# A hybrid state-space and attention layer: TensorE in program order through the projections, turns and parameter products put off by two units

## The chip, the core and the metric

The kernel runs on one core of a Trainium2 chip. The core's engines are TensorE (PE in the rows below, with PEld for its weight loads), VectorE (DVE), ScalarE (ACT), GpSimd (POOL) and SyncE (SP), which here issues DMA transfers only. They run side by side and wait for each other by semaphores; each takes its own instructions in order. The metric is the device time of one launch in microseconds (us).

## What is computed

One layer over 1024 latent tokens and 256 context tokens of width 1024. The normed and modulated input goes through one projection to Q, K, V, U and the gates. U feeds an S5 branch (a complex diagonal state-space model in 32 groups of 16 channels, scanned in both directions), Q, K and V a differential attention with 8 heads. The two branches are merged by the gates, then a gated MLP with a depthwise convolution follows. Cut to what matters here:

```python
z = modulate(x, p['norm1_w'], sh1, sc1) @ w_in
q = rms_norm(z[..., Q_OFF:K_OFF].reshape(b, l, N_HEADS, 2, HEAD_DIM), p['q_norm_w'])
k = rms_norm(z[..., K_OFF:V_OFF].reshape(b, l, N_HEADS, 2, HEAD_DIM), p['k_norm_w'])
v, u, g = ...                       # V_OFF:U_OFF, U_OFF:G_OFF, G_OFF:
q, k = rope_2d(q, rope), rope_2d(k, rope)
y_attn = diff_head_out(blocked_latent_diff_attention(q, k_all, v_all, lam), ...)
y_s5, y_s5_c = s5_branch(u, uc, p, update_ctx)   # discretise, scan, C s + D u, GELU, GLU
x = x + ga1 * merge_branches(g, y_s5, y_attn, p['b_gate'], p['w_out'])
x = x + ga2 * conv_ffn(modulate(x, p['norm2_w'], sh2, sc2), ...)
```

## The kernel before

The part that the change touches is the first third of the program, `phase_a` and what follows it up to the scores of the attention (about 760 us). It works in **units**: `project(tt, W)` multiplies one tile of 128 tokens by one slab of 512 columns of the input projection into a PSUM tile `z` (five of them). Every fp32 product is split into a high part and a rest (`whi`, `wlo` for weights, `hTh`, `hTl` for the input), and three products are added, so that a unit is 8 x 3 = 24 matmuls (L417, L418, L419). A slab's weights come by DMA into `wraw` in four quarters; ScalarE makes `whi`, GpSimd `wlo` (L608).

The units come in this order: U (10 tiles), K in two slabs `s` = 0, 1 (20 units), V in two (20), Q in two (16, latent tokens only). After a unit of K or Q, `qk_post` does the norm and the rotation: ScalarE squares, VectorE reduces over each head (L653), takes a root in a few small steps (L654 to L661) and forms two products with the tables (L665, L669), GpSimd adds them and scales a part, ScalarE scales the rest (L675, L676), and then TensorE **turns** the result: 8 transpositions into `ta` and `tb` (L680).

Between units, three other pieces of work are stepped on as generators. `gates` makes the gates in 32 **halves** of 24 matmuls each (L1308 to L1310 through the helper `gemm`; the same lines serve other products). `s5_params` makes, for each of 8 groups q of the S5 branch (`QUADS`), the matrices `ba`, `ca`, `blk`, `dup` on VectorE or GpSimd, transposes `ba` (L863) and multiplies `ca` with `blk` (L881). `s5_scan` is the scan on VectorE (L959 to L962); `s5_states_in` feeds it during V; `ada_part` computes the second and third part of the adaLN vectors in 16 k-steps a group, each of them two products per half, in row groups of 32 (L300).

When Q is done, the remaining gate halves are made in turn with `s5_out_quad` (8 of them), whose results `Yq` are turned and written to DRAM as `Yd`. The S5 branch's end then loads them as `y` (four quarters, one buffer), applies the GELU on ScalarE, splits into `h5h` (VectorE, L1300) and `h5l` (GpSimd, L1301) and multiplies with the GLU weights into `ta` and `tb` (L1308). Then come the scores `sc` from `K` and `q`.

What sets the order: each engine's instructions are ordered at build time by a scheduler that keeps its own timeline of all engines and puts an instruction where it expects it to be ready. It may so shift the turns, gate halves and parameter products of TensorE between the matmuls of units. Program order decides only where the scheduler sees a tie, or where a part is marked as manual. Pools with a number of buffers (the last argument of `self.t`) limit how far a piece may run ahead.

Of the kernel before, what the change touches and what calls it, by code (L numbers as in the profile page):

```python
# [13 lines left out]
OP = mybir.AluOpType  # L14
# [23 lines left out]
QUADS = G // 4  # L38
# [101 lines left out]
class Kern:  # L140
# [149 lines left out]
    def ada_part(self, pool, ps, crep, grp):  # L290

        nc = self.nc
        pa = self.t(ps, [P, 512], "ada", 1)
        for k in range(KT):
            for h in range(2):
                a = self.t(pool, [P, 2, 512], "araw", 2)
                nc.sync.dma_start(a, self.I["ada"][grp - 1, k][:, 2 * h:2 * h + 2])
                for z in range(2):
                    r0 = 32 * (2 * h + z)
                    nc.tensor.matmul(pa[r0:r0 + 32], crep[:, k], a[:, z], start=k == 0, stop=k == KT - 1,  # L300
                                     tile_position=(0, r0))
# [12 lines left out]
        yield  # L314

    def phase_a(self):
# [180 lines left out]
        for tt in range(NKT):  # L497
            u = stage(first[tt] if tt < TA else project(tt, W))
            if tt < NT:
                nc.scalar.dma_start(self.Ud[:, tt], u)  # L500
            else:
                nc.scalar.dma_start(self.Ucd[(tt - NT) * P:(tt - NT + 1) * P], u)
            if tt % 2:
                next(params, None)
        zp, zp_st = self.pool("pk")
        self.rope_tables(zp, "K")
        gates = self.gates(wp, ps, hTh, hTl)
        for s in (0, 1):
            W = self.load_slab(wp, s)
# [6 lines left out]
        zp_st.close()  # L516
        for _ in params:
            pass
        xp, xp_st = self.pool("s5x")
        states = self.s5_states_in(xp, ps)  # L520
        next(states)
        scan = self.s5_scan()
        for s in (2, 3):
            W = self.load_slab(wp, s)
            for tt in range(NKT):
                v = stage(project(tt, W))
                nc.scalar.dma_start(self.Vd[tt][:, (s - 2) * 512:(s - 1) * 512], v)
                if s > 2 or tt > 1:
                    if next(states, True):
                        next(scan, None)  # L530
        hc_st.close()
        ap_, ap_st = self.pool("pada", "right")
        zp, zp_st = self.pool("pq")
        self.rope_tables(zp, "Q")
        adas = (st for grp in (1, 2) for st in self.ada_part(ap_, ps, crep, grp))
        for s in (5, 6):
            W = self.load_slab(wp, s)
            for tt in range(NT):
# [5 lines left out]
                next(scan, None)  # L544
# [6 lines left out]
        for _ in gates:  # L551
            next(adas, None)
            if nq < QUADS:
                if nq % 2 == 0:
                    Yq = self.t(yp, [P, NT, P], "Yq", 1)
                with self.tc.high_priority():
                    self.s5_out_quad(yp, ps, nq, Yq, xp)
                    nq += 1
                    if nq % 2 == 0:
                        self.s5_transpose(yp, ps, Yq, nq // 2 - 1)  # L560
                if nq == QUADS:
                    for _ in adas:
                        pass
                    ap_st.close()
                    yp_st.close()
                    xp_st.close()
                    tail = self.s5_tail(ps)
            else:
                next(tail, None)
# [43 lines left out]
    def rope_tables(self, zp, kind):  # L613

        nc, I = self.nc, self.I
        tp, tp_st = self.pool("rope")
        cs = self.t(tp, [P, 2, NT, HD], "cossin")
# [13 lines left out]
        tp_st.close()  # L631
# [14 lines left out]
    def qk_post(self, zp, ps, pz, kind, hs, tt):  # L646
# [15 lines left out]
        t1 = self.t(zp, [P, 8, HD], "t1", 2)  # L662
        if tt < NT:
            ct, st = self.tabs[kind]
            nc.vector.tensor_tensor(t1, zv, ct[:, None, tt].to_broadcast([P, 8, HD]), op=OP.mult)  # L665
            t2 = self.t(zp, [P, 8, 2, 32], "t2", 2)
# [9 lines left out]
        nc.gpsimd.tensor_tensor(t1[:, na:], t1[:, na:], r[:, na:, None].to_broadcast([P, 8 - na, HD]), op=OP.mult)  # L676
        pt = self.pst([P, 4, P])
# [93 lines left out]
    def s5_params(self, ps):  # L771
# [62 lines left out]
        for q in range(QUADS):  # L834
            yield
            E = nc.vector if q % 2 or q == 6 else nc.gpsimd
            gs = slice(4 * q, 4 * q + 4)
            sb = self.t(sp, [P, 2, 4, GC], "sb", 1)
            sc = self.t(sp, [P, 2, 4, GC], "sc", 1)
# [7 lines left out]
            ba = self.t(sp, [P, 2, 4, 8, GC], "ba", 1)  # L847
            ca = self.t(sp, [P, 2, 4, 8, GC], "ca", 1)
# [10 lines left out]
            nc.sync.dma_start(self.Wod[q], ca.rearrange("p i g s c -> p i g (s c)"))  # L859
            for i in range(2):  # L860
                pt = self.t(ps, [P, 4, P], "ada", 1)
# [6 lines left out]
            blk = self.t(sp, [P, 2, 2, 4, 2, GC], "blk", 1)  # L868
            nc.gpsimd.memset(blk, 0.0)
            dup = self.t(sp, [P, 2, 4, 2, GC], "dup", 1)  # L870
            V.tensor_copy(dup, bb[:, :, :, None].to_broadcast([P, 2, 4, 2, GC]))
            for d_ in range(2):
                rs = slice(64 * d_, 64 * d_ + 64)
                V.tensor_copy(blk[rs, d_], bb[rs, :, :, None].to_broadcast([64, 2, 4, 2, GC]))
            V.tensor_scalar(sc[:, 1], sc[:, 1], -1.0, None, op0=OP.mult)
            pk = self.t(ps, [P, 272], "ada", 1)
# [12 lines left out]
            nc.sync.dma_start(self.Td[q], kq)  # L889
        sp_st.close()  # L890
# [681 lines left out]
```

## Time and profile before

| | us |
|---|---|
| median of 3 runs (lowest, highest) | 2135.11 (2131.05, 2136.24) |
| the profiled execution, its span | 2132.76, 2131.0 |
| TensorE busy in the span | 2045.3 (96%) |
| VectorE, GpSimd, ScalarE busy | 1161.1, 825.9, 785.5 |
| mean granted TensorE clock | 0.987 of full speed |

A share of busy time is a mean over stages with different limits, so the stages are read one at a time below. Busy time of TensorE counts a matmul that runs at half clock as busy for twice as long; the granted clock beside it tells which it was.

### The profile page before, as it was taken

What the parts mean: (1) busy time and instruction counts of PE and PEld (TensorE: products, weight loads), DVE (VectorE), ACT (ScalarE), POOL (GpSimd) and SP (SyncE); (2) the same over time, 40 slices, a digit from 0 to 9 for tenths busy, and PEclk for the clock granted to TensorE, in tenths of its full rate; (3) what the DMA queues carried; (4) which work ended last, traced back from release to release, by engine and by line L of the source; (5) the groups of instructions that cost most, each with busy time, mean ns of one, the idle gap of its engine ahead of it and who ended that gap; (6) DMA issues with size and microseconds to landing.
All of it is one profiled execution on the core that took longest, in us unless ns stands there. A gap on an engine that the chain in (4) does not pass through costs nothing. (4 is left out here: it accounts for less than half of the span.)

```text
span 2131.0 us, 28111 instructions
## 1 busy us (share of the span) xinstructions
PE 2045.3 (96%) x10656; PEld 1684.9 (79%) x10656; DVE 1161.1 (54%) x1949; ACT 785.5 (37%) x1381; POOL 825.9 (39%) x923
## 2 busy tenths in 40 slices
PE   7989999999899969999999989999999999999998
PEld 4767778866677757999999878878888888888887
DVE  6997953699742144888888653443323323233233
ACT  4345454223331222788888601332112212112121
POOL 1467430144430151466666646433323323223221
PEclk9999999999999979999999999999999999999999
DMA  9335574343566655322321145111111111111102
GB/s 325 111 107 141 156 207 132 114 136 118 158 201 205 209 160 181 94 78 85 114 78 53 35 157 183 51 45 50 52 47 50 46 44 45 47 53 45 50 15 99
DMA packets 150504, 227.83 MB, mean 107 GB/s; under 512 B 27104, under 2 KB 85856, under 8 KB 150368
## 3 DMA queue, kind: packets, MB, share of 16 engines
q1 hardware_dynamic: 140288, 207.67, 32.2%
q10 hardware_dynamic: 10080, 18.35, 2.3%
q8 instruction: 84, 1.38, 0.3%
q14 instruction: 52, 0.43, 0.1%
HBM read 168.76 MB, written 57.21 MB: 106 GB/s over the span
## 5 line engine op out<-in xcount | busy, mean ns | idle before, releaser
L1309 PE MATMUL up<-act,whi 128*128 128x512 f32 x704 | 276.5, 393 | 2.3 <-POOL act L1462 2.1
L1308 PE MATMUL up<-act,whi 128*128 128x512 f32 x704 | 276.1, 392 | 0.0
L1310 PE MATMUL up<-act,wlo 128*128 128x512 f32 x704 | 275.0, 391 | 0.0
L1296 POOL TENSOR_TENSOR wlo<-wraw,whi 128x1024 fp32r<-128x1024 f32 (+1 forms) x64 | 141.4, 2210 | 300.8 <-ACT whi L1295 271.2
L1548 DVE SCALAR_TENSOR_TENSOR y<-up,small,y 128x896 f32<-128x896 f32 (+1 forms) x176 | 124.0, 746 | 237.7 <-ACT y L1543 235.9
L1283 DVE TENSOR_REDUCE mx<-sc 128x1 f32<-128x1280 f32 x128 | 190.9, 1491 | 52.7 <-PE sc L1282 51.8
L417 PE MATMUL z<-whi,hTh 128*128 128x512 f32 x448 | 181.1, 406 | 3.6 <-ACT hTh L406 3.6
L419 PE MATMUL z<-whi,hTl 128*128 128x512 f32 x448 | 177.9, 398 | 0.0
L418 PE MATMUL z<-wlo,hTh 128*128 128x512 f32 x448 | 177.9, 398 | 0.0
L1036 ACT ACTIVATE e<-sc,mx 128x1280 f32<-128x1280 f32 x128 | 171.8, 1342 | 14.3 <-DVE mx L1283 12.6
L1295 ACT CAST whi<-wraw 128x1024 fp32r<-128x1024 f32 (+1 forms) x64 | 61.9, 969 | 311.1 <-PE up L1309 156.8
L1081 PE MATMUL ta<-V,at 128*128 128x128 f32 x1280 | 168.1, 275 | 0.7 <-ACT at L1070 0.7
L1525 DVE SCALAR_TENSOR_TENSOR x<-z,modT,x 128x512 f32<-128x512 f32 x72 | 53.6, 750 | 203.5 <-PE z L1310 203.5
L1309 PEld LDWEIGHTS up<-act,whi 128*128 128x128 f32 x704 | 132.2, 188 | 32.2 <-POOL act L1462 3.4
L1081 PEld LDWEIGHTS ta<-V,at 128*128 128x128 f32 x1280 | 155.5, 191 | 1.0 <-ACT at L1070 0.9
L1308 PEld LDWEIGHTS up<-act,whi 128*128 128x128 f32 x704 | 132.2, 188 | 29.8 <-DVE act L1460 0.2
L1310 PEld LDWEIGHTS up<-act,wlo 128*128 128x128 f32 x704 | 132.2, 188 | 28.7
L1281 PE MATMUL sc<-K,q 128*128 128x512 f32 (+1 forms) x384 | 149.4, 389 | 2.8 <-DMA q<-Qd 2.1
L1282 PE MATMUL sc<-K,q 128*128 128x512 f32 (+1 forms) x384 | 133.2, 361 | 2.9 <-DMA q<-Qd 2.9
L1296 POOL TENSOR_TENSOR wdlo<-wdraw,wdhi 128x512 fp32r<-128x512 f32 (+1 forms) x40 | 56.3, 1409 | 183.4 <-ACT wdhi L1295 183.3
L1309 PE MATMUL z<-gt,wdhi 128*128 128x512 f32 x320 | 124.6, 389 | 1.0 <-POOL gt L1301 1.0
L1310 PE MATMUL z<-gt,wdlo 128*128 128x512 f32 x320 | 124.3, 389 | 0.0
(449 smaller groups left out, 4592.3 us busy)
## 6 DMA issues: line engine op xcount, KB each, us to landing
wraw<-in_wup_dram SPq DMA_DIRECT2D x44, 512.0 KB
araw<-in_ada_dram SPq DMA_DIRECT2D x32, 512.0 KB
q<-Qd SPq DMA_DIRECT2D x128, 128.0 KB
wraw<-in_win_dram SPq DMA_DIRECT2D x28, 512.0 KB
Kd<-st SPq DMA_DIRECT2D x80, 128.0 KB
K<-Kd SPq DMA_DIRECT2D x16, 640.0 KB
aw<-in_ada_dram SPq DMA_DIRECT2D x16, 512.0 KB
wraw<-in_wg_dram SPq DMA_DIRECT2D x16, 512.0 KB
```

Source lines behind the costliest of these rows:

```text
L417: nc.tensor.matmul(pz, hh, wh, start=k == 0, stop=False)
L418: nc.tensor.matmul(pz, hh, wl, start=False, stop=False)
L419: nc.tensor.matmul(pz, hl, wh, start=False, stop=k == KT - 1)
L1036: nc.scalar.activation(em, S[i]["sc"][m][:, :LK], AF.Exp, bias=S[i]["mx"][:, m:m + 1], accum_out=S[i]["l1"] if m else S[i]["l0"])
L1081: nc.tensor.matmul(PO[p][:, j * P:j * P + P], AT[p, kt // 2][:, kt % 2, j * P:j * P + P], W[:, kt], start=kt == 0, stop=kt == NKT - 1)
L1281: nc.tensor.matmul(sc[:, a:b], Q[0][:, m, qs], K[m][:, a:b], start=True, stop=False)
L1282: nc.tensor.matmul(sc[:, a:b], Q[1][:, m, qs], K[m][:, a:b], start=False, stop=True)
L1283: nc.vector.tensor_reduce(S["mx"][:, m:m + 1], sc[:, :LK], axis=AX.X, op=OP.max, negate=True)
L1296: nc.gpsimd.tensor_tensor(l, raw, r32(h), op=OP.subtract)
L1308: mm(o, W[0][:, k], ah[k], start=k == 0, stop=False)
L1309: mm(o, W[0][:, k], al[k], start=False, stop=False)
L1310: mm(o, W[1][:, k], ah[k], start=False, stop=k == n - 1)
```

## The change

1. The code from U to the end of Q runs under `manual_schedule(engines={ET.PE})`: TensorE takes its instructions in the order in which the program is written. The other engines are scheduled as before.
2. `qk_post` no longer turns its result but gives back a function (`qk_turn`). `unit` keeps these in a list and calls the oldest when more than LAG = 2 are there. So unit n's turn stands behind unit n + 2.
3. `s5_params` is cut into `vec(q)`, the elementwise part, and `mul(q)`, TensorE's part, which is called one step later. It is stepped once per unit of K, starting with K, where it began among the units of U. Its tiles `sb`, `sc`, `ba`, `ca`, `blk`, `dup` get two buffers, and some of its PSUM comes from `z`.
4. Gate halves are asked for at other units, and there are 5 of them among the Q units instead of 8. `ada_part` loads both halves of a k-step, yields, and then does the four products in a row. The states begin after three V units instead of two, the scan is stepped in another pattern, and among the `s5_out_quad` steps `adas` is stepped once more.
5. The rotation tables are loaded into a `wraw` buffer, `t1` has three buffers, `t2` one.

```diff
+            aw = []
             for h in range(2):
                 a = self.t(pool, [P, 2, 512], "araw", 2)
                 nc.sync.dma_start(a, self.I["ada"][grp - 1, k][:, 2 * h:2 * h + 2])
+                aw.append(a)
+            yield
+            for h in range(2):
                 for z in range(2):
                     r0 = 32 * (2 * h + z)
-                    nc.tensor.matmul(pa[r0:r0 + 32], crep[:, k], a[:, z], start=k == 0, stop=k == KT - 1,
+                    nc.tensor.matmul(pa[r0:r0 + 32], crep[:, k], aw[h][:, z], start=k == 0, stop=k == KT - 1,
                                      tile_position=(0, r0))
-                yield
+            yield
...
+        LAG = 2
+        later = []
+
+        def unit(part=None):
+
+            if part is not None:
+                later.append(part)
+            if len(later) > LAG or (part is None and later):
+                later.pop(0)()
+
         gates = self.gates(wp, ps, hTh, hTl)
...
-                self.qk_post(zp, ps, project(tt, W), "K", s, tt)
-                if tt in (1, 2, 5, 6):
-                    next(gates)
-                if tt % 4 == 3:
+                for tt in range(NKT):
+                    unit(self.qk_post(zp, ps, project(tt, W), "K", s, tt))
+                    if tt in (1, 3, 5, 6):
+                        next(gates)
                     next(params, None)
...
-                self.qk_post(zp, ps, project(tt, W), "Q", s - 5, tt)
-                if tt in (1, 2, 4, 5):
+                for tt in range(NT):
+                    unit(self.qk_post(zp, ps, project(tt, W), "Q", s - 5, tt))
+                    if tt in (2, 4):
+                        next(scan, None)
+                        next(gates)
+                        next(adas, None)
+                    next(adas, None)
                     next(scan, None)
-                    next(gates)
+                    if tt % 2:
+                        next(scan, None)
+            next(gates)
+            while later:
+                unit()
                 next(adas, None)
...
+        return lambda: self.qk_turn(zp, t1, kind, hs, tt)
...
+        prev = None
+        for q in range(QUADS + 1):
+            yield
+            cur = vec(q) if q < QUADS else None
+            yield
+            if prev:
+                mul(q - 1, *prev)
+            prev = cur
```

How this moves instructions is seen at three places. The first is GpSimd (POOL) at the first K slab; `wlo` are lower halves of weights (L608 before, L635 after, for the slab; L588 for a gate), `ca` and `bb` belong to the parameters of q = 0. Before:

```order
L608 TENSOR_TENSOR wlo_1501<-wraw_1498,whi_1500 128x1024
L608 TENSOR_TENSOR wlo_1507<-wraw_1504,whi_1506 128x1024
L608 TENSOR_TENSOR wlo_1513<-wraw_1510,whi_1512 128x1024
L764 TENSOR_TENSOR ca_938<-pout_909,sc_925 128x512
L767 TENSOR_TENSOR ca_938<-pout_909,sc_925 128x512
L588 TENSOR_TENSOR wlo_1643<-wraw_1640,whi_1642 128x1024
L764 TENSOR_TENSOR bb_928<-fz_856,sb_924 128x64
```

After:

```order
L635 TENSOR_TENSOR wlo_1130<-wraw_1127,whi_1129 128x1024
L793 TENSOR_TENSOR ca_1099<-pout_909,sc_1086 128x512
L796 TENSOR_TENSOR ca_1099<-pout_909,sc_1086 128x512
L635 TENSOR_TENSOR wlo_1136<-wraw_1133,whi_1135 128x1024
L635 TENSOR_TENSOR wlo_1142<-wraw_1139,whi_1141 128x1024
L793 TENSOR_TENSOR bb_1089<-fz_856,sb_1085 128x64
L796 TENSOR_TENSOR bb_1089<-fz_856,sb_1085 128x64
```

Two products that need `pout`, a result of VectorE, now stand between the second quarter of the slab and the third and fourth.

The second place is TensorE behind the third K unit, whose `z` is z_1674 before and z_1313 after; `ba` and `ca` are the parameters of q = 0, `t` are rotated K tiles, L1308 is a gate. Before:

```order
L419 MATMUL z_1674<-whi_1512,hTl_27_113 128x512
L863 MATMUL ada_953<-ident_74,ba_937 128x128 x4
L680 MATMUL tb_1565<-ident_74,t_304_1553 128x128 x4
L680 MATMUL ta_1627<-ident_74,t_314_1615 128x128
L417 MATMUL z_1674<-whi_1512,hTh_20_106 128x512
L418 MATMUL z_1674<-wlo_1513,hTh_20_106 128x512
L680 MATMUL ta_1627<-ident_74,t_314_1615 128x128
L419 MATMUL z_1674<-whi_1512,hTl_28_114 128x512
L680 MATMUL ta_1627<-ident_74,t_314_1615 128x128 x2
L1308 MATMUL z_1736<-hTh_13_99,whi_1642 128x512
```

After:

```order
L423 MATMUL z_1313<-whi_1141,hTl_28_114 128x512
L709 MATMUL tb_1362<-ident_74,t_238_1182 128x128 x4
L903 MATMUL ada_1375<-ident_74,ba_1098 128x128 x4
L903 MATMUL z_1383<-ident_74,ba_1098 128x128 x4
L912 MATMUL z_1391<-ca_1099,blk_1114 32x128 x16
L912 MATMUL z_1391<-sc_1086,dup_1116 32x16 x8
L421 MATMUL z_1420<-whi_1123,hTh_13_99 128x512
L422 MATMUL z_1420<-wlo_1124,hTh_13_99 128x512
L423 MATMUL z_1420<-whi_1123,hTl_21_107 128x512
L421 MATMUL z_1420<-whi_1123,hTh_14_100 128x512
```

Before, turns and the transposition of `ba` stand among the last matmuls of the unit, and the products with `ca` (L881) come 37 rows further down, in the middle of the next unit. After, turn 1, the transpositions and the products with `ca` (L912) stand in one piece, and the fourth unit behind them.

The third place is SyncE's DMA queue ahead of the first scores; `y` are the quarters of the S5 branch's result (the third and fourth of them before, the second to fourth after). Before:

```order
L1321 DMA y_1192_6477<-Yd 128x1024
L1257 DMA K_6892<-Kd 128x1280
L1257 DMA K_6894<-Kd 128x1280
L1260 DMA V_6896<-Vd 128x10x128
L1270 DMA q_6899<-Qd 64x512
L1271 DMA q_6899<-Qd 64x512
L1270 DMA q_6899<-Qd 64x512
L1271 DMA q_6899<-Qd 64x512
L1270 DMA q_6904<-Qd 64x512
L1321 DMA y_1193_6482<-Yd 128x1024
```

After:

```order
L1361 DMA y_1179_6371<-Yd 128x1024
L1334 DMA wraw_6594<-in_wglu_dram 128x512
L1334 DMA wraw_6698<-in_wglu_dram 128x512
L1361 DMA y_1180_6376<-Yd 128x1024
L1361 DMA y_1181_6381<-Yd 128x1024
L1334 DMA wraw_6818<-in_wbs_dram 128x512
L1334 DMA wraw_6828<-in_wbs_dram 128x512
L1297 DMA K_6962<-Kd 128x1280
L1297 DMA K_6964<-Kd 128x1280
L1300 DMA V_6966<-Vd 128x10x128
L1334 DMA wraw_6930<-in_wbs_dram 128x512
L1310 DMA q_6969<-Qd 64x512
```

The third and fourth `y` now follow each other, ahead of K, V and `q`; before, the fourth was in the middle of the `q` loads. An adaLN load stood right ahead of the first `y` before; after, four loads of the S5 output stand there. On TensorE the gate halves left behind the last `Yq` are 188 matmuls after and 105 before, and they stand between the products with `h5h`.

## Rows read from the trace of the kernel before

**Rows 1.** The page's busy time of each engine over the span.

```profile
PE 2045.3 (96%) x10656; PEld 1684.9 (79%) x10656; DVE 1161.1 (54%) x1949; ACT 785.5 (37%) x1381; POOL 825.9 (39%) x923
```

**Rows 2.** Windows: length, busy time of each engine, granted clock, DMA share, GB/s.

```profile
100.00:150.00 50.00, 40.33 (x215) 31.75 (x214) 46.27 (x110) 19.43 (x40) 30.24 (x34) 0.90 0.40 110
...
200.00:250.00 50.00, 44.24 (x287) 34.86 (x286) 43.04 (x84) 25.78 (x62) 29.46 (x24) 0.97 0.58 153
400.00:560.00 160.00, 146.69 (x631) 110.57 (x631) 158.53 (x272) 43.78 (x62) 60.22 (x31) 0.98 0.38 121
```

**Rows 3.** Timeline of PE at the ends of the first K unit.

```profile
96.51 0.39 PE L417 MATMUL z<-whi,hTh 128*128 128x512 f32 x1
...
101.97 0.39 PE L419 MATMUL z<-whi,hTl 128*128 128x512 f32 x1
```

**Rows 4.** Timeline of POOL, 93 to 137 us.

```profile
93.76 7.22 POOL L608 TENSOR_TENSOR wlo<-wraw,whi 128x1024 fp32r<-128x1024 f32 x3 [14.08 <-ACT whi L607]
103.14 1.11 POOL L764 TENSOR_TENSOR ca<-pout,sc 128x512 f32<-128x512 f32 x1 [2.15 <-DVE pout L833]
...
133.62 1.29 POOL L769 TENSOR_TENSOR ca<-ca,tq 128x512 f32<-128x512 f32 x1
```

**Rows 5.** Timeline of DVE, 93 to 126 us.

```profile
93.80 2.52 DVE L765 TENSOR_TENSOR ptmp<-pw 128x128 f32<-128x128 f32 x1
...
101.17 0.29 DVE L768 TENSOR_TENSOR ptmp<-pw 128x128 f32<-128x128 f32 x1
...
102.77 0.29 DVE L833 COPY pout<-pw 64x256 f32<-64x256 f32 x1
...
116.68 0.68 DVE L653 TENSOR_REDUCE qv<-sq 128x8 f32<-128x512 f32 x1
```

**Rows 6.** Waits of PE, 100 to 300 us, summed by line and releaser.

```profile
PE tb L680 <- ACT t L675: 7.5, 3, 4.0
```

**Rows 7.** Window of 4 us behind the longest of these waits.

```profile
126.00:130.00 4.00, 4.00 (x13) 2.65 (x14) 3.08 (x5) 3.97 (x12) 3.84 (x5) 0.50 0.00 0
```

**Rows 8.** Groups of DVE by line, 400 to 560 us: the scan.

```profile
L962 DVE TENSOR_TENSOR X<-X,sc 128x640 f32<-128x640 f32 (+2 forms) x47 | 35.7, 760 | 1.0
L959 DVE TENSOR_TENSOR sc<-X,Apa 128x640 f32<-128x640 f32 (+2 forms) x47 | 35.4, 754 | 0.4
L961 DVE TENSOR_TENSOR X<-X,sc 128x640 f32<-128x640 f32 (+2 forms) x47 | 32.5, 691 | 0.0
L960 DVE TENSOR_TENSOR sc<-X,Apb 128x640 f32<-128x640 f32 (+2 forms) x47 | 30.6, 651 | 0.0
```

**Rows 9.** Groups of PE by line, 400 to 560 us: transpositions of units.

```profile
L680 PE MATMUL ta<-ident,t 128*128 128x128 f32 x16 | 3.0, 320 | 4.4 <-POOL t L676 4.4
```

**Rows 10.** Timeline of PE at two adaLN steps.

```profile
448.76 1.05 PE L300 MATMUL ada<-araw,crep 128*32 128x512 f32 x4
...
691.24 1.06 PE L300 MATMUL ada<-araw,crep 128*32 128x512 f32 x8
```

**Rows 11.** Waits of PE, 745 to 770 us.

```profile
PE tb L1308 <- DVE h5h L1300: 3.9, 1, 3.9
PE sc L1282 <- DMA q<-Qd: 2.9, 1, 2.9
```

**Rows 12.** Window of the same stretch.

```profile
745.00:770.00 25.00, 14.55 (x43) 9.91 (x42) 5.07 (x5) 7.86 (x10) 6.23 (x4) 0.66 1.01 303
```

**Rows 13.** Timeline of SP, the DMA queue, 715 to 760 us.

```profile
717.32 2.20 SPq L297 DMA_DIRECT2D araw<-in_ada_dram  x2
719.61 0.39 SPq L1321 DMA_DIRECT2D y<-Yd  x1
...
753.88 0.33 SPq L1321 DMA_DIRECT2D y<-Yd  x1
```

**Rows 14.** Timeline of DVE, 715 to 765 us.

```profile
731.52 0.69 DVE L1300 CAST h5h<-y 128x1024 fp32r<-128x1024 f32 x1 [2.96 <-ACT y L1322]
...
761.52 0.69 DVE L1300 CAST h5h<-y 128x1024 fp32r<-128x1024 f32 x1 [10.09 <-ACT y L1322]
```

More of the change, by code (lines that the diff above doesn't have):

```diff
@@ L495, in stage @@
             return x
[L497 to L506, printed above, removed]
+        LAG = 2
[5 more added lines that the diff above has]
+                later.pop(0)()
@@ L507, in phase_a @@
         gates = self.gates(wp, ps, hTh, hTl)
-        for s in (0, 1):
-            W = self.load_slab(wp, s)
+        with self.tc.manual_schedule(engines={ET.PE}):
             for tt in range(NKT):
-                self.qk_post(zp, ps, project(tt, W), "K", s, tt)
-                if tt in (1, 2, 5, 6):
-                    next(gates)
-                if tt % 4 == 3:
-                    next(params, None)
[L516 to L525, printed above, removed]
-                v = stage(project(tt, W))
-                nc.scalar.dma_start(self.Vd[tt][:, (s - 2) * 512:(s - 1) * 512], v)
-                if s > 2 or tt > 1:
+                u = stage(first[tt] if tt < TA else project(tt, W))
+                if tt < NT:
+                    nc.scalar.dma_start(self.Ud[:, tt], u)
+                else:
+                    nc.scalar.dma_start(self.Ucd[(tt - NT) * P:(tt - NT + 1) * P], u)
@@ new lines, in phase_a @@
+            zp, zp_st = self.pool("pk")
+            self.rope_tables(zp, wp, "K")
+            next(params)
+            for s in (0, 1):
+                W = self.load_slab(wp, s)
+                for tt in range(NKT):
+                    unit(self.qk_post(zp, ps, project(tt, W), "K", s, tt))
+                    if tt in (1, 3, 5, 6):
+                        next(gates)
+                    next(params, None)
+            W = self.load_slab(wp, 2)
+            for tt in range(3):
+                v = stage(project(tt, W))
+                nc.scalar.dma_start(self.Vd[tt][:, 0:512], v)
+                if later:
+                    unit()
@@ new lines, in phase_a @@
+            zp_st.close()
+            for _ in params:
+                pass
+            xp, xp_st = self.pool("s5x")
+            states = self.s5_states_in(xp, ps)
+            next(states)
+            scan = self.s5_scan()
+            for s in (2, 3):
+                if s > 2:
+                    W = self.load_slab(wp, s)
+                for tt in range(3 if s == 2 else 0, NKT):
+                    v = stage(project(tt, W))
+                    nc.scalar.dma_start(self.Vd[tt][:, (s - 2) * 512:(s - 1) * 512], v)
@@ L529, in phase_a @@
                     if next(states, True):
                         next(scan, None)
[L531 to L538, printed above, removed]
-                self.qk_post(zp, ps, project(tt, W), "Q", s - 5, tt)
-                if tt in (1, 2, 4, 5):
-                    next(scan, None)
-                    next(gates)
+            hc_st.close()
@@ new lines, in phase_a @@
+            ap_, ap_st = self.pool("pada", "right")
+            zp, zp_st = self.pool("pq")
+            self.rope_tables(zp, wp, "Q")
+            adas = (st for grp in (1, 2) for st in self.ada_part(ap_, ps, crep, grp))
+            for s in (5, 6):
+                W = self.load_slab(wp, s)
+                for tt in range(NT):
[5 more added lines that the diff above has]
+                    next(adas, None)
+                    next(scan, None)
+                    if tt % 2:
+                        next(scan, None)
@@ L543, in phase_a @@
+            next(gates)
+            while later:
+                unit()
                 next(adas, None)
-                next(scan, None)
         zp_st.close()
@@ L553, in phase_a @@
             if nq < QUADS:
+                next(adas, None)
                 if nq % 2 == 0:
@@ L630, in rope_tables @@
         self.tabs = {kind: (ct, s_)}
-        tp_st.close()
     def lam(self, zp):
@@ L676, in qk_post, with qk_turn @@
         nc.gpsimd.tensor_tensor(t1[:, na:], t1[:, na:], r[:, na:, None].to_broadcast([P, 8 - na, HD]), op=OP.mult)
+        return lambda: self.qk_turn(zp, t1, kind, hs, tt)
+    def qk_turn(self, zp, t1, kind, hs, tt):
+        nc = self.nc
         pt = self.pst([P, 4, P])
@@ L833, in s5_params, with vec @@
             V.tensor_copy(pout[64:128, i], pw[64:128, i, 1:9])
-        for q in range(QUADS):
-            yield
+        def vec(q):
             E = nc.vector if q % 2 or q == 6 else nc.gpsimd
             gs = slice(4 * q, 4 * q + 4)
-            sb = self.t(sp, [P, 2, 4, GC], "sb", 1)
-            sc = self.t(sp, [P, 2, 4, GC], "sc", 1)
+            sb = self.t(sp, [P, 2, 4, GC], "sb", 2)
+            sc = self.t(sp, [P, 2, 4, GC], "sc", 2)
             nc.sync.dma_start(sb, I["sb"][:, :, gs])
@@ L846, in s5_params @@
             tq = self.t(sp, [P, 4, 8, GC], "tq", 1)
-            ba = self.t(sp, [P, 2, 4, 8, GC], "ba", 1)
-            ca = self.t(sp, [P, 2, 4, 8, GC], "ca", 1)
+            ba = self.t(sp, [P, 2, 4, 8, GC], "ba", 2)
+            ca = self.t(sp, [P, 2, 4, 8, GC], "ca", 2)
             def bc(z, i):
@@ L859, in s5_params, with mul @@
             nc.sync.dma_start(self.Wod[q], ca.rearrange("p i g s c -> p i g (s c)"))
+            blk = self.t(sp, [P, 2, 2, 4, 2, GC], "blk", 2)
+            nc.gpsimd.memset(blk, 0.0)
+            dup = self.t(sp, [P, 2, 4, 2, GC], "dup", 2)
+            V.tensor_copy(dup, bb[:, :, :, None].to_broadcast([P, 2, 4, 2, GC]))
+            for d_ in range(2):
+                rs = slice(64 * d_, 64 * d_ + 64)
+                V.tensor_copy(blk[rs, d_], bb[rs, :, :, None].to_broadcast([64, 2, 4, 2, GC]))
+            V.tensor_scalar(sc[:, 1], sc[:, 1], -1.0, None, op0=OP.mult)
+            return ba, ca, blk, dup, sc
+        def mul(q, ba, ca, blk, dup, sc):
             for i in range(2):
-                pt = self.t(ps, [P, 4, P], "ada", 1)
+                pt = self.t(ps, [P, 4, P], "z", 5) if i else self.t(ps, [P, 4, P], "ada", 1)
                 for g in range(4):
@@ L866, in s5_params @@
                 nc.sync.dma_start(self.Wid[q][:, i], wi)
[L868 to L876, printed above, removed]
+            pk = self.t(ps, [P, 272], "z", 5)
             for o, w, x in ((0, blk[:, 0], ca), (P + GC, blk[:, 1], ca), (P, dup, sc)):
```

9 lines of the change are left out of this document (4 added, 5 removed).

## The prediction

> **What bounds the kernel now.** I read the page first: TensorE is busy for 2045.3 us, 96% of the span, and no other engine comes near [rows 1]. So only two things can move the time: work that TensorE is spared, and the stretches where it stands. I then went through the span in windows of 50 us to find those, and read the waits of PE there. Up to the scores of the attention (about 760 us) there are four places. (a) The start of the K units, 100 to 150 us: 40.33 us busy of 50 at a granted clock of 0.90 [rows 2], where a transposition waits for the scale that ScalarE applies [rows 6]. That scale waits for the root chain on VectorE, whose first K reduction comes only at 116.68 us [rows 5]. (b) The second K slab, 200 to 250 us: 5.8 us idle [rows 2]. (c) From 400 to 560 us, the scan: VectorE is busy for 158.53 of 160 us and TensorE for 146.69 [rows 2]; the reader is to see that in this stretch VectorE is the bound and TensorE has 13 us to spare. Four scan lines take 35.7 + 35.4 + 32.5 + 30.6 = 134.2 us of it [rows 8]. (d) The tail of the first phase, 745 to 770 us: 43 records of matmuls in 25 us at a mean clock of 0.66 [rows 12], with waits for h5h and for q [rows 11].
>
> The unit of counting is a projection unit or a gate half, 24 matmuls: 24 steps from 96.51 to 101.97 us [rows 3], 5.46 us.
>
> **The change, part by part.** The matmuls of the projections, the gates and the transpositions stay the same in number. Four things move.
>
> *Start of K.* Before, POOL makes the three missing lower halves of the first K slab in one go, 93.76 to 100.98 us, and only then begins the S5 parameters at 103.14 us [rows 4]. After, two parameter products on ca stand ahead of the second and third of these halves, and they wait for pout. If pout came when it comes before (102.77 + 0.29 = 103.06 us [rows 5]), the last half would be there 2.2 + 4.8 us later, at 110.1 us, and the first unit would end 8 matmuls' worth later still, near 111.5, not 101.97 us: 9.6 us lost. But the same rows show VectorE's small products at 2.52 us while POOL runs these halves and at 0.29 us as soon as they are over [rows 4, 5]. After, POOL stands from 96.2 us on, so two or three of those products shrink by 2.2 us each and pout comes at about 98.5 us; then 98.5 + 2.2 + 4.8 = 105.5, and the unit ends at about 107.0 us: 5.0 us lost. I take 5.0 (bounds 0 and 9.6). The Trainium skill (GPSIMD Engine Reference, section 1, Specifications) says that GpSimd shares its SBUF interfaces with VectorE and that instructions with two SBUF inputs contend; by it the sum has the 5.0, without it the 9.6, and the two timelines agree with the page.
>
> *First transposition and first parameter product.* Before, the scheduler puts the first parameter's transposition, the turns of two units and a whole gate half into whatever gap there is, and the products on ca only in the middle of the fourth unit. After, everything is in one line: unit 3, turn 1, product 0, unit 4. Product 0 needs the negated ca. Its last POOL step runs at 133.62 to 134.9 us before [rows 4]; after, the chain starts 4.6 us earlier (98.5 for 103.1) but has a gate's lower half (2.4 us) in it, so about 133, and 1.5 us of negation on VectorE: 134.5 to 135.5 us. TensorE is at turn 1 at 107.0 + 3 x 5.46 = 123.4 us, when its scale is ready or nearly so. So it stands for some 11 us, and its clock falls: before, after the idle 118 to 126 us, the window from 126 has a clock of 0.50 [rows 7], which is the lower level, 1.2 GHz. That costs another 3 us (about 6 us of work at half rate). Before, the same stretch loses 9.7 us of idleness and 10% of 50 us of clock [rows 2], 14.7 together. So nothing is gained or lost here (bounds -5 and +5): the wait for the scale is replaced by one for ca.
>
> *Rest of K.* The parameters now start with the K units and their vector part is called at every other unit, so VectorE's work is packed towards the front. Its posts for units 9 and 10 come late, and the turns behind them are in line: I count 3, 2 and 10 us of standing there, and as much as 3 us of clock, against about 12 us that the rest of K loses now. Beyond that the LAG of two units covers everything. K together: +5.0 (start) + 0 + 2 to 6, less what the later units give back; I take **+5** (bounds -4 and +14). In the V units the states begin one unit later, and their short transpositions wait in line where they were slipped in: **+3** (bounds 0 and +6).
>
> *Q under the scan.* VectorE is full from the scan's start, S, for 160 us whatever TensorE does, so turn 9 comes at about S + 160 before and after. What counts is the work that TensorE can do in these 160 us. After, in line before turn 9: 7 V units, 11 Q units, 2 gate halves, 20 x 5.46 = 109.2; 7 adaLN steps of 1.05 [rows 10], 7.4; 8 turns in two halves of which 16 records of one take 3.0 us [rows 9], under 3. That makes 119 us, so 41 us stand idle, where it is 13.3 idle and 0.02 x 160 = 3.2 of clock now [rows 2]. The cover was five gate halves; three of them are moved behind, and turns that were late let other work pass. The falls of the clock behind these waits lie under VectorE's cover, all but the last. So **+24.5** (bounds +12, if the turns come earlier because POOL and ScalarE are less pushed, and +30).
>
> *adaLN steps.* A step with two of the four row groups takes 1.05 us, 4 records; one where all four stand together takes 1.06 us, 8 records [rows 10]. So what is paired costs half. Now there are 29 groups, after, in TensorE's order, 19: 10 x 1.0 = **-10** (bounds -5, if the pairs don't run beside each other in the line, and -12).
>
> *Tail.* The gate halves put off now stand between the four h5 products: after the last transposition of Yq 188 gate matmuls are left, 42.7 us, where it is 105 now, 23.8 us. The y loads stand ahead of the loads of K, V and q in SP's queue, and the first is no longer behind an adaLN load whose issue ended at 719.5 us (717.32 + 2.20), just ahead of it [rows 13]. The four casts to h5h run from 731.52 to 761.52 us, 10 us apart [rows 14]; if the first comes some 5 us sooner behind the last Yq, the fourth is there 37 to 40 us behind it, just when TensorE gets to it. What goes is 25 us less 47 matmuls (43 recorded [rows 12], and four that seem missing) of 0.2275: 25 - 10.7 = 14.3 us; I take **-14** (bounds -6, if the chain of the four y keeps its own pace, and -16).
>
> **The sum.** From the scan's start on that is 24.5 - 10 - 14 = +0.5. Counted the other way, along TensorE's new line from turn 9 to the fourth h5 product, I get 199 us where it is 207 us now, and turn 9 a microsecond later: -7. The two differ by what the short instructions cost between others; I take the middle, -3. With K and V it is +5 + 3 - 3 = +5 on the profiled execution's 2132.8 us: 2138. The three runs have a median of 2135.1 us, so that the change is 3 to 5 us, under the 0.3% (6.4 us) that is about what a measurement of this kernel can tell from no change. The forecast is **2138 us, no change to speak of**: what the tail and the adaLN steps give is eaten by turns in line under the scan and at the start of K.
>
> **The rivals.** *Slower: the clock.* The in-line turns make seven or so standstills of 8 to 17 us (turn 1 and product 0, turn 10 in K; turns 1, 4, 6 and 9 in Q), and each is followed by a stretch at half rate as in [rows 7]. If the 41 us of idleness in Q are instead 41 plus clock that isn't under VectorE's cover (3 us each, four times), and K loses its upper bound, it is +5 + 9 + 9: 2156 us. It decides from the point where turn 9 comes after S + 165. The Trainium skill (TensorE: Matmul & The Clock Gate, HAM oscillation) says that gaps in TensorE's work put its clock to half rate and that the price is paid after each gap; the trace agrees with its 0.50, and the rule speaks against this change. Against the rival: most of it lies under a VectorE that is full anyway. *Faster: VectorE is sooner through.* If turn 9 comes at S + 150, because POOL's products and the scan collide less (the four scan lines, alike in count and shape, have means from 651 to 760 ns [rows 8]), and K's start costs nothing, it is +5 - 10 - 5 - 5: 2118 us. For it: the tail's stall is real and its cover is certain by the order. Against: nothing in the change touches the scan's work. *The tail's gain doesn't come.* The scores need K and q, whose loads are now behind the last y load, which waits for the third h5l; now that y load goes at 753.88 us, between the q loads [rows 13]. If the scores wait 12 us for them, 2150 us. TensorE has work until 50 us after the last Yq and the loads should be there at 45, so I don't expect it.
>
> **How the numbers follow.** No change (2129 to 2141): 0.34. Slower: the clock 0.22, the tail 0.07, sums of small terms 0.07: 0.36. Faster: VectorE 0.18, small terms 0.12: 0.30. The likeliest one's own range is 2129 to 2141. For 8 in 10 I leave out a tenth at either end: the faster case at 2118 and the slower one at 2156 lie inside: 2114 to 2157.
>
> **What would show it.** K: POOL's second lower half of the first slab starts near 101 and the first unit ends at 107; wait of the ca products (L912) for the negation about 11 us. Q: waits of the turns (L709) of about 40 us in the 160 after the scan's start, and VectorE still at 98% there. adaLN: groups of 8 records at about 1.06 us. Tail: no wait for h5h over 3 us, and a clock of 0.9 or more in the windows before the scores. The prediction is wrong if turns under the scan wait much less than 25 us, or if the loads of K and q end the tail.

## The result: 0.5% slower

The changed kernel takes 2145.73 us (median of 4 runs, 2144.16 to 2146.11), the kernel before 2134.2 us (4 runs, 2131.05 to 2136.24). The ratio is 1.0054, with a 95% interval of 1.0036 to 1.0071: 11.5 us slower. The forecast was 2138 and no change; the time lies in its range of 2114 to 2157, but above the 2129 to 2141 of its likeliest case, on the side of the slower ones.

I cut both traces at six events that the change does not touch in itself: the last U matmul on a context tile, the same for K, the first product of the scan, the last turn of Yq, the first product of the up-projection, and the end. (These are differences of start times in the timelines, not rows of a view. Each column but the last two is the length of a stretch, the first from the start of the span. "K to scan" includes the V units before the scan's start.) The kernels of the experiments stand in the same table; the last two columns are gate matmuls recorded behind the last Yq turn, and the median time. The profiled execution of f2 ran at a mean clock of 0.934 and took 2133.76 us, 9 above its median, so its row is somewhat long.

```
us                        U end     K  K to scan  scan to Yq  Yq to up   rest  gates    time
before                     96.3 204.1      100.1       314.7     535.2  880.7    105  2134.2
after                     101.1 212.1      106.7       313.9     527.5  881.0    188  2145.7
e1_u_free                 100.4 213.0      105.6       312.5     529.6  880.4    188  2142.4
e2_scheduler               98.6 208.8      104.5       291.3     529.1  880.9    188  2115.0
e3_before_pairs            97.4 204.5       99.0       308.8     535.5  879.8    100  2130.6
e4_before_gates            99.1 205.0      100.0       299.1     527.8  879.8    178  2110.2
e5_gates_pairs             99.5 202.6       98.0       304.5     521.1  879.8    143  2108.8
e7_line_8gates            100.6 213.1      104.3       326.1     526.7  879.6     93  2153.1
e8_line_lag4q             101.1 214.1      105.4       316.6     522.6  879.7    131  2140.4
e9_3gates_pairs            96.8 205.0       99.9       300.5     526.8  880.1    177  2112.6
f2_line_ukv               101.4 213.8      105.1       295.0     530.6  886.1    188  2124.9
f3_line_q                  99.1 208.6      104.8       312.4     528.6  881.0    188  2135.6
```

So 4.8 + 8.0 + 6.6 us are lost up to the scan's start, and 0.8 + 7.7 come back behind it. The page of the changed kernel shows that TensorE's busy time went down, by 7 us against [rows 1], while the span went up:

```profile
span 2142.4 us, 28075 instructions
...
PE 2037.9 (95%) x10656; PEld 1691.0 (79%) x10656; DVE 1157.4 (54%) x1949; ACT 774.1 (36%) x1373; POOL 816.8 (38%) x923
```

It is the time in which TensorE stands that grew. Windows of the changed kernel, in the columns of [rows 2] and [rows 12], with the scan's 160 us from its own start:

```profile
100.00:150.00 50.00, 37.44 (x201) 29.77 (x200) 45.02 (x93) 16.92 (x37) 39.07 (x40) 0.86 0.33 93
200.00:250.00 50.00, 39.22 (x242) 30.34 (x231) 45.49 (x97) 22.32 (x57) 24.13 (x19) 0.90 0.57 159
419.90:579.90 160.00, 128.13 (x560) 97.26 (x559) 158.64 (x278) 32.54 (x52) 56.62 (x32) 0.91 0.39 120
745.00:770.00 25.00, 25.00 (x110) 20.46 (x109) 2.08 (x3) 5.31 (x7) 11.06 (x7) 1.00 0.41 136
```

Under the scan VectorE is as full as before (158.64 of 160), and TensorE's idle time went from 13.3 to 31.9 us, its clock from 0.98 to 0.91. In the tail it is the other way round: 110 records of matmuls in 25 us at full clock, where there were 43 at 0.66.

What the line waits for, the waits of PE of the changed kernel from 100 to 310 us, then from 400 to 620 us, then from 745 to 860 us:

```profile
PE z L422 <- POOL wlo L635: 6.7, 5, 3.2
PE z L912 <- POOL ca L795: 4.2, 1, 4.2
PE z L912 <- DVE ca L886: 4.1, 1, 4.1
PE tb L709 <- ACT t L700: 3.8, 1, 3.8
...
PE z L903 <- POOL ba L798: 1.7, 1, 1.7
...
PE ta L709 <- POOL t L701: 15.2, 2, 8.7
PE tb L709 <- POOL t L701: 10.0, 2, 9.6
PE z L422 <- POOL wlo L635: 6.0, 1, 6.0
PE ta L311 <- ACT stage L308: 2.7, 1, 2.7
...
PE tb L1348 <- DVE h5h L1340: 2.6, 1, 2.6
```

The reader is to see three kinds: turns that wait for their scaled tile (15.2 + 10.0 = 25.2 us under the scan, where it was 8.9 + 4.4 = 13.3), the first parameter products (ba and ca, 10 us), and a kind that the prediction put at the start of K alone: a new slab's lower half, `wlo`, for the first unit of a slab (L422). In the line the rest of the unit and what follows it wait with it. Of the 13.3 us before, [rows 9] has the 4.4; the others, 400 to 560 us:

```profile
PE tb L680 <- POOL t L676: 8.9, 3, 4.3
```

(A turn is four transpositions, into `ta` or `tb` by turns, and not eight; in Q GpSimd scales the whole tile, so a late turn there waits mostly for POOL.)

The longest wait also costs clock. It stands at turn 9, and windows of 4 us around it follow:

```profile
578.30 1.12 PE L709 MATMUL tb<-ident,t 128*128 128x128 f32 x4 [9.63 <-POOL t L701]
```

```profile
568.00:572.00 4.00, 0.67 (x3) 0.21 (x2) 4.00 (x8) 1.07 (x3) 0.00 (x0) 1.00 0.78 176
572.00:576.00 4.00, 0.00 (x0) 0.00 (x0) 4.00 (x8) 0.31 (x2) 1.26 (x1) 0.74 0.85 282
576.00:580.00 4.00, 1.70 (x6) 1.58 (x7) 4.00 (x9) 0.93 (x2) 1.98 (x2) 0.50 0.00 1
580.00:584.00 4.00, 4.00 (x11) 3.07 (x10) 2.87 (x9) 1.53 (x3) 2.72 (x3) 0.50 0.46 131
```

The engine comes back at the lower level, 1.2 GHz, as in [rows 7].

### The profile page after: what moved, and what is told of

It reads as the page before. It is cut to its first block, busy times and chain, and to the rows that moved or that the text cites. A ratio compares the mean times of both kernels' runs of the same rounds, so it can differ in the third digit from the quotient of the medians.

```text
span 2142.4 us, 28075 instructions
## 1 busy us (share of the span) xinstructions
PE 2037.9 (95%) x10656; PEld 1691.0 (79%) x10656; DVE 1157.4 (54%) x1949; ACT 774.1 (36%) x1373; POOL 816.8 (38%) x923
## 5 line engine op out<-in xcount | busy, mean ns | idle before, releaser
L422 PE MATMUL z<-wlo,hTh 128*128 128x512 f32 x448 | 180.2, 402 | 13.5 <-POOL wlo L635 13.5
```

Source lines behind the costliest of these rows:

```text
L422: nc.tensor.matmul(pz, hh, wl, start=False, stop=False)
```

## The experiments

The theory after the result: program order on TensorE is what costs, most of it under the scan, because a turn or a slab that is not ready stops all units behind it. The first expectation, that of e2, put its net cost at 12 to 20 us; the runs put it at 31. The rival: the order is harmless and the other parts (turns put off, split parameters, fewer halves under Q) cost the time.

**e2_scheduler: all of the change but the order.**

```diff
-        with self.tc.manual_schedule(engines={ET.PE}):
+        if True:
             for tt in range(NKT):
```

> The changed kernel without program order on TensorE: all its other parts (turns given back as functions, split parameters, doubled buffers, five gate halves under Q, paired adaLN steps) stay. My theory (the line is what costs 19 us up to the scan's start and as much as 25 us under the scan, and it also carries the gain in the tail): the scan starts by 404 us, the idle time in the 160 us behind it falls below 25 us, the wait for h5h is back, and the time is 2126 to 2134. Rival (the longer lag, the split of the parameters or the three missing gate halves cost the time themselves): 2140 or more.

Measured: 2115.01 us, ratio to before 0.9908 (0.9896 to 0.9921), 31 us below the changed kernel. The rival is out, and TensorE's idle time under the scan falls to 15.5 us as expected, but the theory had the size too small: it is 11 us faster than the 2126 to 2134 expected. Two details are wrong: the scan starts at 411.9, not by 404 us, so that other parts of the change cost time there too (below), and the wait for h5h does not come back (2.6 us, as in the changed kernel). The 188 gate matmuls stand in the tail without the order too, so the order does not carry the gain there. Its window under the scan and that of the tail:

```profile
411.90:571.90 160.00, 144.53 (x638) 109.92 (x637) 158.70 (x280) 36.80 (x58) 56.67 (x33) 0.95 0.42 132
745.00:770.00 25.00, 25.00 (x110) 20.32 (x109) 9.71 (x11) 7.82 (x13) 15.27 (x12) 1.00 0.49 163
```

With the same five halves under Q, TensorE now does 638 records of matmuls in the 160 us and not 560: units run ahead of turns that are not ready (turns wait for 13.6 us from 400 to 620 us, in place of 25.2).

**f2_line_ukv and f3_line_q: the order in one part only.** f2 ends the ordered block ahead of Q (the edit below), f3 begins it there.

```diff
+        if True:
             hc_st.close()
             ap_, ap_st = self.pool("pada", "right")
```

> The changed kernel with TensorE in program order in U, K and V only; from the Q units on the scheduler orders it. My theory (of the 31 us that the order costs, some 22 lie under the scan): the stretch from the scan's start to the last turn of Yq is 290 to 296 us long as without any program order, not 314, and the time is 2119 to 2127. Rival (a delay that the order makes in K and V is carried on, and the order in Q itself costs little): 2138 or more.

> The changed kernel with the scheduler's order on TensorE in U, K and V and program order in the Q units only. My theory: K and the way to the scan's start are as long as without any program order (209 and 104.5 us), the stretch from the scan's start to the last turn of Yq is 310 to 316 us, and the time is 2134 to 2140. Rival (program order in K and V is what costs): 2124 or less.

Measured: f2 2124.90 us (0.9967, 0.9957 to 0.9976), f3 2135.57 us (1.0014, 1.0006 to 1.0023). Both as the theory had it, the stretch from the scan to Yq too: 295.0 and 312.4 us. From e2 the order costs 9.9 us in U, K and V and 20.6 us in Q: together 30.5, and the changed kernel is 30.7 above e2. Counted from the kernel before as it ran beside each of them, it is 11.0 and 21.7. Either way a third of the cost lies in U, K and V and two thirds in Q. The waits of PE of f3, 400 to 620 us:

```profile
PE ta L710 <- POOL t L702: 13.4, 2, 13.1
PE tb L710 <- POOL t L702: 9.6, 1, 9.6
PE z L422 <- POOL wlo L636: 5.3, 1, 5.3
PE ada L304 <- DMA araw<-in_ada_dram: 4.4, 1, 4.4
PE ta L311 <- ACT stage L308: 2.4, 1, 2.4
```

**e1_u_free: the order from K on.**

> The changed kernel with TensorE left to the scheduler in the ten U units, in program order from K on. My theory (the line of units makes TensorE wait for the split of the normed input, and this costs 4 us before K begins): the last U unit ends at about 97 us in place of 101, and the time is 4 us below the changed kernel's, about 2141.5. Rival (the late end of U is a matter of the first loads, which differ from run to run): no change, 2145 to 2146.

Measured: 2142.43 us (1.0039, 1.0027 to 1.0051), the time of the theory, but not its place: U ends at 100.4, not at 97 us. Over the profiles of this study U ends at 96.3 to 100.4 us under the scheduler (8 of them) and at 100.6 to 101.4 us in line (4). So the line costs something like 2.5 us in U, and the execution's own start moves by as much. So the theory is not shown by this run, whose interval overlaps that of the changed kernel (1.0036 to 1.0071); it is borne out only in the mean of U's ends.

**e4_before_gates: five gate halves under Q, on the kernel before.** The edit, cut here, also takes over the change's stepping of the scan and of the adaLN steps.

```diff
-                if tt in (1, 2, 4, 5):
+                if tt in (2, 4):
                     next(scan, None)
                     next(gates)
...
             if nq < QUADS:
+                next(adas, None)
```

> The kernel before, its scheduler as it is, with the change's five gate halves in place of eight among the Q units and its extra adaLN step among the S5 outputs. My theory (the tail's stall of 14 us is covered by halves put off, and the scan's stretch pays for it only in part): the wait for h5h shrinks below 4 us, idle time behind the scan's start grows by some 8 us, 4 to 8 us faster than before, about 2128. Rival (what the tail gains, the scan's stretch loses, since VectorE sets its length): 2131 to 2137.

Measured: 2110.22 us, 0.9888 (0.9874 to 0.9903), 24 us faster than before: three times the upper end of what the theory had. Under the scan nothing is paid, since the scheduler lets units run ahead in place of the halves: the window below has 9.9 us idle at a clock of 0.96, where [rows 2] has 13.3 at 0.98. The other pieces of the edit were not tried apart, but the scan itself does not gain by its new stepping: it takes 161.3 us from its first product to its last, 158.9 before. And the tail's cover is about 20 us, not 14: from Yq to the up-projection it is 7.4 us shorter though 73 more gate matmuls (16.6 us) stand in it, in place of three adaLN groups that took 4.2 us there.

```profile
404.10:564.10 160.00, 150.09 (x642) 110.01 (x641) 158.62 (x279) 36.55 (x57) 58.02 (x32) 0.96 0.41 130
740.00:765.00 25.00, 24.46 (x109) 19.83 (x108) 7.60 (x9) 9.44 (x15) 14.15 (x10) 1.00 0.69 223
```

Where the cover lies is seen when one adds up by how much the starts of consecutive matmuls lie further apart than 0.2275 us (gaps of more than 0.05 us alone; an estimate, since some records are missing). In the first 60 us behind the last Yq turn the kernel before loses 18.9 us by that count and e4 0.9. That is more than the 14 us that [rows 12] shows, as some 3 of it go in the first 20 us, among the adaLN groups, and more behind that window. The kernel before has a second stall, behind the GLU, when the split of `gth` into h5h and h5l on VectorE and GpSimd is late (waits of PE, 780 to 802 us):

```profile
PE tb L1308 <- DVE h5h L1300: 4.0, 1, 4.0
PE tb L1309 <- POOL h5l L1301: 1.3, 2, 1.1
```

That one the halves hardly cover: from 60 to 130 us behind the last Yq turn the kernel before loses 11.7 us and e4 still 10.5.

**e3_before_pairs: the paired adaLN steps, on the kernel before.** The edit is the first piece of the diff above.

> The kernel before with one thing of the change alone: an adaLN step loads both halves and then makes its four products in a row. My theory (29 groups become about 20, each 1.0 us, and most stand where TensorE is full): 6 to 9 us faster than before, about 2126. Rival (the steps fill places where TensorE would stand anyway, or the pairs don't run beside each other): within 3 us of before, 2131 to 2137.

Measured: 2130.59 us, 0.9985 (0.9977 to 0.9994): 3.5 us, between theory and rival. A pair does run side by side. In the changed kernel:

```profile
476.35 1.06 PE L304 MATMUL ada<-araw,crep 128*32 128x512 f32 x8
...
521.75 1.94 PE L304 MATMUL ada<-araw,crep 128*32 128x512 f32 x8
```

The first is as in [rows 10], the second fell into a stretch at half clock. In the changed kernel the 19 groups take 23.8 us from start to next start, the 29 of before 29.8: 6.0 us less, not 10, as four of the 19 ran partly at half clock or with a wait in them (1.4 to 3.8 us each, in place of 1.0).

**e5_gates_pairs and e9_3gates_pairs: both on the kernel before, with five and with three halves under Q.**

> The kernel before, its scheduler as it is, with five gate halves under Q and the paired adaLN steps together. My theory (two gains at different places, 24 and 3.5 us, add up; neither the turns' lag nor the split parameters are needed): 2104 to 2109, faster than either alone and below the changed kernel without its program order (2115). Rival (both cover the same idle time, or the lag and the split carry part of that kernel's gain): 2110 to 2116.

> The kernel before with paired adaLN steps and three gate halves under Q, the other 21 behind it. My theory (the tail has little left to cover with 19 halves, 3 us of waits, and units run ahead under the scan as long as z tiles are free): within 4 us of the one with five, 2102 to 2110. Rival (each half moved behind gives what the three before gave, 8 us): 2090 to 2095.

Measured: e5 2108.84 us (0.9878, 0.9865 to 0.9891), e9 2112.56 us (0.9898, 0.9885 to 0.9911). e5 is the fastest, within the theory's bounds, but its 1.4 us below e4 are less than the two intervals can tell: behind the halves, the pairs are worth nothing that shows. e9 is 2.6 us above the theory's bounds, and not at the rival's 2090 to 2095. With 177 matmuls behind Yq it has the cover of e4 (178) and no more (0.7 us are lost in the first 60 us behind the last Yq turn), and under the scan a new wait appears, for a free z (waits of PE of e9, 400 to 620 us):

```profile
PE tb L692 <- POOL t L688: 6.7, 3, 3.9
PE z L421 <- DVE t L681: 4.8, 1, 4.8
```

**e7_line_8gates: eight halves under Q, in line.**

```diff
                     if tt in (2, 4):
                         next(scan, None)
-                        next(gates)
                         next(adas, None)
+                    if tt in (1, 2, 4, 5):
+                        next(gates)
...
-            next(gates)
             while later:
```

> The changed kernel with eight gate halves under Q as before, still in program order. My theory (in a line the halves fill the idle time under VectorE: 16 us of the 32 idle ones in the 160 behind the scan's start go, but the tail loses its cover of about 25): idle time under the scan falls to 15 to 20, the waits for h5h come back, 2146 to 2156. Rival (the three missing halves are the reason that the changed kernel is slow): below 2140.

Measured: 2153.09 us (1.0086, 1.0073 to 1.0099), 7.4 us above the changed kernel: as the theory had it, and the rival is out, though the halves fill only 8 of the 32 idle us (136.30 busy of 160), not 12 to 17. The tail's waits are back (PE, 740 to 860 us):

```profile
PE tb L1348 <- DVE h5h L1340: 7.8, 2, 4.0
PE tb L1349 <- POOL h5l L1341: 2.5, 3, 1.2
PE sc L1322 <- DMA q<-Qd: 2.3, 1, 2.3
PE sc L1321 <- DMA q<-Qd: 2.1, 1, 2.1
```

**e8_line_lag4q: turns of Q put off by four units, in line.**

```diff
+            LAG[0] = 4
...
-        t1 = self.t(zp, [P, 8, HD], "t1", 3)
+        t1 = self.t(zp, [P, 8, HD], "t1", 3 if kind == "K" else 5)
```

> The changed kernel with the turns of Q put off by four units in place of two (five buffers for the rotated tile there), K as it is. My theory (what costs under the scan is that a turn which is not ready stops the units behind it): the waits of turns for the scaled tile, 25 us in 400 to 600, fall below 8, and the time is 2125 to 2136. Rival (VectorE's posts and the five tiles z are the limit, and a unit then waits for its z where it waited for the turn): waits of z take the place, 2141 to 2147.

Measured: 2140.43 us (1.0032, 1.0021 to 1.0043), 5.3 us below the changed kernel, between theory and rival, with an interval that overlaps that of the changed kernel. The waits of turns are gone and z did not take their place, as the theory said; but others in the same line did (PE, 400 to 620 us):

```profile
PE z L422 <- POOL wlo L636: 11.4, 3, 6.2
PE ta L311 <- ACT stage L308: 9.0, 1, 9.0
PE ada L304 <- DMA araw<-in_ada_dram: 1.5, 2, 1.3
```

TensorE is busy for 146.55 of the 160 us, 18 more than in the changed kernel, and only some 5 arrive: 9.0 us go to the adaLN transposition (L311) that waits in line behind its copy, and only 131 gate matmuls stand behind Yq, so that 13 us of cover are missing in the tail, where some 8 us are lost again by the count of e4. The line has one place that waits after another; taking one away uncovers the next.

## Why the prediction was right and wrong

**Start of K.** Right in kind, and in the point that VectorE's products shrink while GpSimd stands: they ran at 0.28 and 0.29 us from 94.3 us on, where [rows 5] has 2.52, and pout was there at 96.9, earlier than the 98.5 foreseen. But GpSimd stood for another reason than the one given: not for pout, which was there first, but for ScalarE's `whi`, until 98.58 us. A row of VectorE, then GpSimd's:

```profile
94.27 0.29 DVE L794 TENSOR_TENSOR ptmp<-pw 128x128 f32<-128x128 f32 x1
...
98.58 2.42 POOL L635 TENSOR_TENSOR wlo<-wraw,whi 128x1024 fp32r<-128x1024 f32 x1 [33.72 <-ACT whi L634]
100.96 1.55 POOL L793 TENSOR_TENSOR ca<-pout,sc 128x512 f32<-128x512 f32 x1
102.48 1.56 POOL L796 TENSOR_TENSOR ca<-pout,sc 128x512 f32<-128x512 f32 x1
103.99 4.68 POOL L635 TENSOR_TENSOR wlo<-wraw,whi 128x1024 fp32r<-128x1024 f32 x2
...
135.07 1.27 POOL L798 TENSOR_TENSOR ca<-ca,tq 128x512 f32<-128x512 f32 x1
```

The order of the halves is as read, but U ended later, so the wait for them is 2.6 us and not 5.0.

**First parameter product.** Right: ca's last GpSimd step ends at 136.3 us (133 foreseen), and TensorE waits 10 us there for ba and ca, with a clock of 0.50 behind it (138 to 142 us), in place of the waits of before.

**U, K and V.** Mis-sized: +8 was foreseen for K and V and nothing for U; it was 4.8 + 8.0 + 6.6 = 19.4. The step that failed is "Beyond that the LAG of two units covers everything", and that U has no term in the sum. Two causes, by the table: the order (f2 against e2, 9.9 us, with waits for the first `wlo` of a slab and for the parameters), and other parts of the change, which make K and the way to the scan 4 to 5 us longer each even under the scheduler (208.8 and 104.5 us in e2, 208.6 and 104.8 in f3, against 202.6 to 205.0 and 98.0 to 100.1 where those parts are absent). Which of these parts (the split, the later start, the doubled buffers, the states one unit later) does it stays open, as they were not tried apart.

**Q under the scan.** Right in mechanism; the idle time was put at 41 us and came to 31.9, with more clock lost than I allowed for. Together that is 31.9 + 0.09 x 160 = 46 us for 13.3 + 3.2 before: +30 by that count. By the table it is +25: from the scan to Yq it is 0.8 us shorter, with 83 gate matmuls (18.9 us) moved out and 7 adaLN groups fewer. I took +24.5. The waits of turns, put at about 40 us, are 25.2, at the very bound below which the prediction called itself wrong; the rest of the 31.9 is a slab's `wlo` (6.0) and `whi` (0.7).

**adaLN.** The term of -10 was too large: 6.0 us in the changed kernel, 3.5 alone.

**Tail.** Too small: -14 for the first stall, and -22 came: 7.7 us less from Yq to the up-projection with 18.9 us more of gates in it, less the 4.2 us of adaLN groups that had stood there. The four h5h come in the order foreseen and a little sooner, the first 10 us after Yq and the last 35, not 37 to 40:

```profile
743.41 0.69 DVE L1340 CAST h5h<-y 128x1024 fp32r<-128x1024 f32 x1 [28.39 <-ACT y L1362]
...
768.29 0.69 DVE L1340 CAST h5h<-y 128x1024 fp32r<-128x1024 f32 x1 [7.68 <-ACT y L1362]
```

About half of what was missed lies in the first 60 us behind Yq: 18.9 us are lost there by the count of e4, and 0.1 in the changed kernel, where the prediction had counted the 25 us of [rows 12] alone. The other half is the second stall (e4 above), which shrinks in part, from 11.7 to 7.1 us. Its 20 us in the kernel before, then in the changed kernel:

```profile
780.00:790.00 10.00, 7.83 (x33) 5.52 (x31) 9.72 (x8) 2.52 (x5) 10.00 (x8) 1.00 0.09 29
790.00:800.00 10.00, 6.54 (x16) 4.26 (x17) 7.14 (x7) 0.54 (x1) 8.44 (x6) 0.66 0.10 26
...
800.00:810.00 10.00, 7.16 (x24) 5.08 (x25) 9.90 (x8) 1.32 (x2) 10.00 (x7) 0.83 1.03 302
810.00:820.00 10.00, 9.71 (x43) 7.45 (x42) 4.48 (x6) 3.97 (x6) 3.91 (x4) 1.00 0.77 230
```

The rival of late loads of K and q did not come: no wait for q stands between 745 and 860 us.

**The sum.** Foreseen +5 + 3 - 3 = +5, measured +19.4 - 8.2 = +11.2 in spans. The sections ahead of the scan came 11 us worse than foreseen and the rest 5 us better, so that the time is nearer to the forecast than its terms are: that much is luck. The rival "slower: the clock" names the right direction, with standstills that do lower the clock. Of its two additions the upper bound of K came about (17 us for K and V by it, 14.6 measured), the clock outside VectorE's cover did not: turn 9 came 158.4 us after the scan's start, and not after 165.

## What to carry to other kernels

Program order on an engine is only as good as the piece that is least ready: before fixing it, list for each instruction that may wait what stands behind it, the first instruction of each new weight block too. Work put off to where an engine is known to stand is worth having by itself; here an edit of a few lines, three gate halves and the steps around them, gave 24 us on the kernel before, and the halves alone 7 us inside the fixed order. When a change has several parts, put each on the old kernel alone: two of its parts made it faster than either version (2108.8 us).

## What the runs showed of the hardware

VectorE and GpSimd slow each other in both directions. GpSimd's 128x512 product on pout and sc took 1.11 us [rows 4], and 1.55 us from 100.96 us of the changed kernel on, where a VectorE product of the same kind, 1.59 us long, ran beside it. Another such VectorE product took 2.91 us beside a `wlo` of GpSimd; in the kernel before, with GpSimd idle, they took 0.64 to 0.69 us. The Trainium skill (GPSIMD Engine Reference, section 1, Specifications) has the two engines share their SBUF interfaces and contend when a VectorE instruction has two SBUF inputs; the trace agrees, with longer times on both sides. VectorE's rows in the changed kernel:

```profile
98.63 2.91 DVE L793 TENSOR_TENSOR ca<-pout,sc 128x512 f32<-128x512 f32 x1
101.47 1.59 DVE L796 TENSOR_TENSOR ca<-pout,sc 128x512 f32<-128x512 f32 x1
```

The products of an adaLN step cost the same for four row groups of 32 as for two, 1.0 us from start to next start where nothing disturbs them; that this is worth little in the end (3.5 us alone, where 6 to 9 were expected) was the surprise.
